# RMSNorm and projection on one core: bf16 cast on GpSimd, bf16 transposes on TensorE, four token tiles per transfer, a software pipeline over pairs of tiles

## The chip, the cores and the metric

The kernel runs on one core of one Trainium2 chip. A core has five engines that run side by side, each with its own instruction queue that is worked off in order: TensorE (PE: matmuls and transposes through its array; weight loads, PEld, overlap them), VectorE (DVE), ScalarE (ACT), GpSimd (POOL), and SyncE (SP), which here only issues DMAs. Sixteen DMA engines move data between HBM and the on-chip memory SBUF; TensorE writes its results to PSUM, from which VectorE and ScalarE read. The metric is the device time of the program in microseconds (us), the median of several runs. A profile of one execution gives a span, the time from the first to the last instruction.

## The reference

```python
batch, seq, dim, out_dim = 16, 1024, 512, 768
rms = np.sqrt(np.mean(x ** 2, axis=-1, keepdims=True) + eps)
x_norm = x / rms * gamma
return np.matmul(x_norm, weight).astype(np.float32)
```

There are 16,384 tokens of 512 f32 values (33.6 MB), a weight of 512x768 f32 (1.57 MB) and an output of 16,384x768 f32 (50.3 MB).

## The kernel before

The tokens are cut into 128 tiles of 128 tokens, one token per partition. Gamma is multiplied into the weight once, which is kept in bf16 as `w_bf` (L56 to L61: SyncE loads both, ScalarE multiplies). The division by the root mean square commutes with the matmul, so it is applied at the end, as the scale `rstd` of each output row.

The loop over tiles (L64 to L95) does this for each tile. SyncE loads `xt_f`, 128x512 f32, 256 KB, 2 KB per partition (L66). ScalarE squares it and accumulates the row sum in `ssq` (L70), and takes the root (L73); VectorE takes the reciprocal (L75). TensorE transposes the tile in four pieces of 128x128, in f32, to PSUM (L80); ScalarE and VectorE in turn copy each piece to SBUF as bf16, `xT` (L81). TensorE multiplies with the weight in two column blocks of 384, four steps in the contracted dimension each (L88). ScalarE scales the first block with `rstd` into `ot` (L94), VectorE the second (L92). SyncE stores `ot`, 384 KB, 3 KB per partition (L95).

The order within each engine's queue is chosen by the scheduler of the tile framework, which interleaves neighbouring tiles. Pools set how far tiles may run ahead: three input tiles (`xin`), three outputs (`outp`), four PSUM tiles for transposes, two for matmul results. All DMAs are issued from SyncE's one queue, in which a DMA that waits for its data or its buffer holds up those behind it.

Of the kernel before, what the change touches and what calls it, by code (L numbers as in the profile page):

```python
# [1 line left out]

# [6 lines left out]
_cc.warn_once_per_call_stack = lambda *a, **k: None  # L9
if hasattr(_cc, "log"):  # L10
    _cc.log.warn_once_per_call_stack = lambda *a, **k: None

F32 = mybir.dt.float32
BF16 = mybir.dt.bfloat16
AF = mybir.ActivationFunctionType


@with_exitstack
def kernel(
    ctx: ExitStack,  # L20
    tc: tile.TileContext,
    x: bass.AP,
    gamma: bass.AP,
    weight: bass.AP,
    eps: float,
    out: bass.AP,
):
    nc = tc.nc
    P = 128

    x = x.flatten_outer_dims()
    out = out.flatten_outer_dims()
    N, D = x.shape
    _, O = out.shape
    K = D // P

    wk = weight.rearrange("(ko ki) o -> ki ko o", ki=P)
    gk = gamma.rearrange("(ko ki) -> ki ko", ki=P)

    singles = ctx.enter_context(tc.tile_pool(name="singles", bufs=1))  # L40
    xin = ctx.enter_context(tc.tile_pool(name="xin", bufs=3))
    work = ctx.enter_context(tc.tile_pool(name="work", bufs=3))
    stats = ctx.enter_context(tc.tile_pool(name="stats", bufs=4))
    xt_pool = ctx.enter_context(tc.tile_pool(name="xt", bufs=3))
    tpsum = ctx.enter_context(tc.tile_pool(name="tpsum", bufs=4, space=bass.MemoryType.PSUM))
    opsum = ctx.enter_context(tc.tile_pool(name="opsum", bufs=2, space=bass.MemoryType.PSUM))
    outp = ctx.enter_context(tc.tile_pool(name="out", bufs=3))

    ident = singles.tile([P, P], F32)
    make_identity(nc, ident)  # L50

    eps_sb = singles.tile([P, 1], F32)
    nc.vector.memset(eps_sb, float(eps))  # L53

    w_f32 = singles.tile([P, K, O], F32)
    nc.sync.dma_start(out=w_f32, in_=wk)  # L56
    g_sb = singles.tile([P, K], F32)
    nc.sync.dma_start(out=g_sb, in_=gk)
    w_bf = singles.tile([P, K, O], BF16)
    for k in range(K):  # L60
        nc.scalar.mul(out=w_bf[:, k, :], in_=w_f32[:, k, :], mul=g_sb[:, k:k + 1])  # L61

    ntiles = N // P
    for m in range(ntiles):  # L64
        xt_f = xin.tile([P, D], F32)
        nc.sync.dma_start(out=xt_f, in_=x[m * P:(m + 1) * P, :])  # L66

        xs = work.tile([P, K, P], BF16)
        ssq = stats.tile([P, 1], F32)
        nc.scalar.activation(out=xs, in_=xt_f.rearrange("p (ko ki) -> p ko ki", ki=P),  # L70
                             func=AF.Square, accum_out=ssq)
        rms = stats.tile([P, 1], F32)
        nc.scalar.activation(out=rms, in_=ssq, func=AF.Sqrt, scale=1.0 / D, bias=eps_sb)  # L73
        rstd = stats.tile([P, 1], F32)
        nc.vector.reciprocal(out=rstd, in_=rms)  # L75

        xT = xt_pool.tile([P, K, P], BF16)
        for k in range(K):
            tp = tpsum.tile([P, P], F32)
            nc.tensor.transpose(out=tp, in_=xt_f.rearrange("p (ko ki) -> p ko ki", ki=P)[:, k, :], identity=ident)  # L80
            nc.vector.tensor_copy(out=xT[:, k, :], in_=tp) if k % 2 else nc.scalar.copy(out=xT[:, k, :], in_=tp)  # L81

        ot = outp.tile([P, O], F32)
        OT = 384
        for oi in range(O // OT):
            ops = opsum.tile([P, OT], F32)
            for k in range(K):
                nc.tensor.matmul(out=ops, lhsT=xT[:, k, :], rhs=w_bf[:, k, oi*OT:(oi+1)*OT],  # L88
                                 start=(k == 0), stop=(k == K - 1))
            oslc = ot[:, oi*OT:(oi+1)*OT]  # L90
            if oi % 2:
                nc.vector.tensor_single_scalar(out=oslc, in_=ops, scalar=rstd, op=mybir.AluOpType.mult)  # L92
            else:
                nc.scalar.mul(out=oslc, in_=ops, mul=rstd)  # L94
        nc.sync.dma_start(out=out[m * P:(m + 1) * P, :], in_=ot)  # L95


# [1 line left out]
_INS = ['x', 'gamma', 'weight', 'eps']  # L99
_OUTS = [((16, 1024, 768), 'float32')]  # L100
#: Inputs that are plain numbers.
_NUMBERS = {'eps': 9.999999747378752e-06}


# [26 lines left out]
```

## Time and profile before

| what | us |
|---|---|
| median of 3 runs | 299.18 |
| the runs | 299.02, 299.18, 301.84 |
| span of the profiled execution | 300.5 |
| TensorE busy | 256.5 (85%) |
| ScalarE busy | 239.1 (80%) |
| VectorE busy | 151.9 (51%) |
| GpSimd busy | 0.7 (0%) |

The page gives each engine's busy time, the DMA queues, and the costliest groups of instructions with their count and mean duration. Other views of the trace give waits by engine and line, the instructions in order of time, and busy time and DMA rate in chosen stretches. Matmuls are pipelined, so a matmul's duration holds latency that the next one overlaps; its cost is read from how far apart the starts of several are. The DMA share is the mean busy share of the 16 DMA engines.

### The profile page before, as it was taken

The numbers are of one execution on the slowest core, as the hardware profiler recorded it, in microseconds if no ns is written. First come the engines' busy times: TensorE is split into PE (matmuls) and PEld (weight loads), VectorE is DVE, ScalarE is ACT, GpSimd is POOL, SyncE is SP. The second block draws the span as 40 slices with busy tenths as digits, with TensorE's granted clock in tenths as the row PEclk, the third lists the DMA queues.
The fourth block names the chain that finished last, engine by engine and source line by source line (L and its number), as shares of the span: only waits on it lengthen the run. The fifth ranks groups of instructions, "written<-read, shape, count | busy, mean of one in ns | idle before, by whom it ended". The sixth has DMA issues, their size and how long they took to land.

```text
span 300.5 us, 5189 instructions
## 1 busy us (share of the span) xinstructions
PE 256.5 (85%) x1536; PEld 153.2 (51%) x1536; DVE 151.9 (51%) x513; ACT 239.1 (80%) x774; POOL 0.7 (0%) x6
## 2 busy tenths in 40 slices
PE   0498799999979999979979989879989889899984
PEld 0155365555545555545545555545555545555542
DVE  0145354646545556546545545645546555556562
ACT  0987569888878888878879878879879879888873
POOL 0000000000000000000000000000000000000000
PEclk9999889999999999999999999999999999999998
DMA  6248869999989999979979989988999999899994
GB/s 230 112 145 277 286 214 318 302 303 314 299 289 323 315 277 327 306 272 312 311 266 306 326 280 301 313 287 292 310 308 285 317 313 303 307 295 305 296 316 164
DMA packets 37948, 85.81 MB, mean 286 GB/s; under 512 B 4640, under 2 KB 4640, under 8 KB 37920
## 3 DMA queue, kind: packets, MB, share of 16 engines
q1 hardware_dynamic: 37920, 85.48, 85.6%
q8 instruction: 12, 0.20, 0.3%
q14 instruction: 16, 0.13, 0.1%
HBM read 35.13 MB, written 50.33 MB: 284 GB/s over the span
## 4 chain that ended last, share of the span: by engine, by line
DMA 46%; PE 43%; ACT 5%; DVE 3%; issue 2%; SPq 1%; ACTq 0%
DMA xt_f<-in_x_dram 44%; PE ops L88 32%; PE tp L80 11%; DVE ot L92 3%; DMA g_sb<-in_gamma_dram 2%; ACT xs L70 1%; ACT ot L94 1%; ACT w_bf L61 1%; ACT rms L73 1%; ACT L73 0%; ACT L61 0%; SPq L95 0%; ACT xT L81 0%; SPq L56 0%; SPq L66 0%
## 5 line engine op out<-in xcount | busy, mean ns | idle before, releaser
L88 PE MATMUL ops<-w_bf,xT 128*128 128x384 bf16 x1024 | 210.2, 330 | 8.3 <-ACT xT L81 4.2
L88 PEld LDWEIGHTS <-xT 128*128 128x128 bf16 x1024 | 98.6, 101 | 70.0 <-ACT xT L81 13.4
L80 PE MATMUL tp<-ident,xt_f 128*128 128x128 f32 x512 | 104.2, 285 | 31.7 <-DMA xt_f<-in_x_dram 31.1
L70 ACT ACTIVATE xs<-xt_f 128x512 bf16<-128x512 f32 x128 | 80.8, 631 | 31.6 <-DMA xt_f<-in_x_dram 30.1
L80 PEld LDWEIGHTS tp<-ident,xt_f 128*128 128x128 f32 x512 | 68.0, 143 | 72.9 <-DMA xt_f<-in_x_dram 45.9
L92 DVE TENSOR_SCALAR ot<-ops,rstd 128x384 f32<-128x384 f32 x128 | 79.1, 618 | 47.8 <-PE ops L88 47.5
L94 ACT ACTIVATE ot<-ops,rstd 128x384 f32<-128x384 f32 x128 | 73.9, 577 | 8.5 <-PE ops L88 2.5
L81 DVE CAST xT<-tp 128x128 bf16<-128x128 f32 x256 | 64.3, 281 | 20.2 <-PE tp L80 19.5
L81 ACT CAST xT<-tp 128x128 bf16<-128x128 f32 x256 | 65.7, 259 | 9.6 <-PE tp L80 2.1
L75 DVE RECIPROCAL rstd<-rms 128x1 f32<-128x1 f32 x128 | 20.9, 163 | 76.5 <-ACT rms L73 76.1
L73 ACT ACTIVATE rms<-ssq,eps_sb 128x1 f32<-128x1 f32 x128 | 37.9, 296 | 0.0
L70 ACT ACTIVATION_READ_ACCUMULATOR xs<-xt_f 128x1 f32 x128 | 24.2, 189 | 0.0
L61 ACT ACT_TABLE_LOAD x1 | 1.3, 1283 | 7.9 <-DMA g_sb<-in_gamma_dram 7.9
L61 ACT ACTIVATE w_bf<-w_f,g_sb 128x768 bf16<-128x768 f32 x4 | 3.4, 922 | 0.0
L73 ACT ACT_TABLE_LOAD x1 | 1.3, 1283 | 0.0
L53 DVE MEMSET eps_sb<- 128x1 f32 x1 | 0.1, 59 | 0.8 <-PEq L112 0.8
masks.py:199 POOL TENSOR_SCALAR_AFFINE_SELECT ident<-ident 128x128 f32<-128x128 f32 x1 | 0.3, 293 | 0.1
masks.py:197 POOL MEMSET ident<- 128x128 f32 x1 | 0.2, 204 | 0.3 <-POOLq L112 0.3
L112 POOL MEMSET const-bfloat16-1.0<- 128x1 bf16 x1 | 0.1, 101 | 0.0
L112 POOL MEMSET const-uint8-127<- 128x1 uint8 x1 | 0.1, 101 | 0.0
L112 POOL MEMSET const-float32-0.0<- 128x1 f32 x1 | 0.1, 98 | 0.2 <-issue 0.2
L112 POOL MEMSET const-float32-1.0<- 128x1 f32 x1 | 0.1, 98 | 0.0
## 6 DMA issues: line engine op xcount, KB each, us to landing
out_dram<-ot SPq DMA_DIRECT2D x128, 384.0 KB, 3.3
xt_f<-in_x_dram SPq DMA_DIRECT2D x128, 256.0 KB, 3.7
w_f<-in_weight_dram SPq DMA_DIRECT2D x1, 1536.0 KB, 6.5
g_sb<-in_gamma_dram SPq DMA_DIRECT2D x1, 2.0 KB, 6.6
```

The source lines that it names most:

```text
L53: nc.vector.memset(eps_sb, float(eps))
L61: nc.scalar.mul(out=w_bf[:, k, :], in_=w_f32[:, k, :], mul=g_sb[:, k:k + 1])
L70: nc.scalar.activation(out=xs, in_=xt_f.rearrange("p (ko ki) -> p ko ki", ki=P), func=AF.Square, accum_out=ssq)
L73: nc.scalar.activation(out=rms, in_=ssq, func=AF.Sqrt, scale=1.0 / D, bias=eps_sb)
L75: nc.vector.reciprocal(out=rstd, in_=rms)
L80: nc.tensor.transpose(out=tp, in_=xt_f.rearrange("p (ko ki) -> p ko ki", ki=P)[:, k, :], identity=ident)
L81: nc.vector.tensor_copy(out=xT[:, k, :], in_=tp) if k % 2 else nc.scalar.copy(out=xT[:, k, :], in_=tp)
L88: nc.tensor.matmul(out=ops, lhsT=xT[:, k, :], rhs=w_bf[:, k, oi*OT:(oi+1)*OT], start=(k == 0), stop=(k == K - 1))
L92: nc.vector.tensor_single_scalar(out=oslc, in_=ops, scalar=rstd, op=mybir.AluOpType.mult)
L94: nc.scalar.mul(out=oslc, in_=ops, mul=rstd)
L112: nc = _bacc.Bacc("TRN2", target_bir_lowering=False, num_devices=1)
```

## The change

A group is now four tiles: partition p holds the four consecutive tokens 4p to 4p+3 of the group's 512, so that a load brings 8 KB in one run per partition (1 MB per DMA) and a store takes 12 KB (1.5 MB). The input pool holds eight groups; the first load is split in two, and the last group is stored in two halves. The order of each queue is the order in which the code is written (`manual_schedule`). Work goes in pairs of tiles, j. GpSimd casts a pair to bf16 (`cast`, L71). ScalarE squares both tiles and takes both roots in one instruction (L77, L80). TensorE transposes the bf16 pair in eight pieces into one bf16 PSUM tile (L90), which VectorE copies in one instruction (L92). The matmuls have column blocks of 512 and 256 (L106); ScalarE scales the first tile's 768 columns (L110), VectorE the second's (L112). In step j of the loop stand: a load six groups ahead (in even steps), the cast of pair j+2, squares and transposes of pair j+1, matmuls and scaling of pair j, and after every second step the store of the group. Gamma is loaded as four rows and transposed on TensorE; the weight is loaded in four DMAs from ScalarE's queue, and VectorE multiplies gamma into it.

```diff
--- before.py
+++ after.py
@@ -33,72 +33,141 @@
     N, D = x.shape
     _, O = out.shape
     K = D // P
+    G = 4
+    NG = N // (P * G)
+    NP = 2 * NG
+    PF = 6
+    SPLITS = [(0, 512), (512, O)]
 
-    wk = weight.rearrange("(ko ki) o -> ki ko o", ki=P)
-    gk = gamma.rearrange("(ko ki) -> ki ko", ki=P)
+
+    xg = x.rearrange("(g p t) d -> g p t d", p=P, t=G)
+    og = out.rearrange("(g p t) o -> g p t o", p=P, t=G)
 
     singles = ctx.enter_context(tc.tile_pool(name="singles", bufs=1))
-    xin = ctx.enter_context(tc.tile_pool(name="xin", bufs=3))
-    work = ctx.enter_context(tc.tile_pool(name="work", bufs=3))
+    xin = ctx.enter_context(tc.tile_pool(name="xin", bufs=PF + 2))
+    xbp = ctx.enter_context(tc.tile_pool(name="xb", bufs=3))
+    junk = ctx.enter_context(tc.tile_pool(name="junk", bufs=2))
     stats = ctx.enter_context(tc.tile_pool(name="stats", bufs=4))
     xt_pool = ctx.enter_context(tc.tile_pool(name="xt", bufs=3))
-    tpsum = ctx.enter_context(tc.tile_pool(name="tpsum", bufs=4, space=bass.MemoryType.PSUM))
-    opsum = ctx.enter_context(tc.tile_pool(name="opsum", bufs=2, space=bass.MemoryType.PSUM))
-    outp = ctx.enter_context(tc.tile_pool(name="out", bufs=3))
+    tpsum = ctx.enter_context(tc.tile_pool(name="tpsum", bufs=2, space=bass.MemoryType.PSUM))
+    opsum = ctx.enter_context(tc.tile_pool(name="opsum", bufs=3, space=bass.MemoryType.PSUM))
+    outp = ctx.enter_context(tc.tile_pool(name="out", bufs=4))
 
-    ident = singles.tile([P, P], F32)
-    make_identity(nc, ident)
+    x_tiles, xb_tiles, rstd_tiles, xT_tiles, o_tiles = {}, {}, {}, {}, {}
 
-    eps_sb = singles.tile([P, 1], F32)
-    nc.vector.memset(eps_sb, float(eps))
+    def load(g, parts=1):
+        xt = xin.tile([P, G, D], F32, name="xt")
+        x_tiles[g] = xt
+        n = G // parts
+        for i in range(parts):
+            nc.sync.dma_start(out=xt[:, i * n:(i + 1) * n, :], in_=xg[g, :, i * n:(i + 1) * n, :])
 
-    w_f32 = singles.tile([P, K, O], F32)
-    nc.sync.dma_start(out=w_f32, in_=wk)
-    g_sb = singles.tile([P, K], F32)
-    nc.sync.dma_start(out=g_sb, in_=gk)
-    w_bf = singles.tile([P, K, O], BF16)
-    for k in range(K):
-        nc.scalar.mul(out=w_bf[:, k, :], in_=w_f32[:, k, :], mul=g_sb[:, k:k + 1])
+    def xpair(j):
+        return x_tiles[j // 2][:, 2 * (j % 2):2 * (j % 2) + 2, :]
 
-    ntiles = N // P
-    for m in range(ntiles):
-        xt_f = xin.tile([P, D], F32)
-        nc.sync.dma_start(out=xt_f, in_=x[m * P:(m + 1) * P, :])
+    def cast(j):
+        xb = xbp.tile([P, 2, D], BF16, name="xb")
+        xb_tiles[j] = xb
+        nc.gpsimd.tensor_copy(out=xb, in_=xpair(j))
 
-        xs = work.tile([P, K, P], BF16)
-        ssq = stats.tile([P, 1], F32)
-        nc.scalar.activation(out=xs, in_=xt_f.rearrange("p (ko ki) -> p ko ki", ki=P),
-                             func=AF.Square, accum_out=ssq)
-        rms = stats.tile([P, 1], F32)
+    def squares(j):
+        ssq = stats.tile([P, 2], F32, name="ssq")
+        for t in range(2):
+            jk = junk.tile([P, D], BF16, name="jk")
+            nc.scalar.activation(out=jk, in_=xpair(j)[:, t, :], func=AF.Square,
+                                 accum_out=ssq[:, t:t + 1])
+        rms = stats.tile([P, 2], F32, name="rms")
         nc.scalar.activation(out=rms, in_=ssq, func=AF.Sqrt, scale=1.0 / D, bias=eps_sb)
-        rstd = stats.tile([P, 1], F32)
+        rstd = stats.tile([P, 2], F32, name="rstd")
         nc.vector.reciprocal(out=rstd, in_=rms)
+        rstd_tiles[j] = rstd
 
-        xT = xt_pool.tile([P, K, P], BF16)
+    def transposes(j):
+        xb = xb_tiles.pop(j)
+        tp = tpsum.tile([P, 2, K, P], BF16, name="tp")
+        for t in range(2):
+            for k in range(K):
+                nc.tensor.transpose(out=tp[:, t, k, :], in_=xb[:, t, k * P:(k + 1) * P], identity=ident)
+        xT = xt_pool.tile([P, 2, K, P], BF16, name="xT")
+        nc.vector.tensor_copy(out=xT, in_=tp)
+        xT_tiles[j] = xT
+
+    def matmuls(j):
+        g, h = j // 2, j % 2
+        if h == 0:
+            o_tiles[g] = outp.tile([P, G, O], F32, name="ot")
+        ot = o_tiles[g]
+        xT = xT_tiles.pop(j)
+        rstd = rstd_tiles.pop(j)
+        for t in range(2):
+            ops = opsum.tile([P, 2, 512], F32, name="ops").rearrange("p a b -> p (a b)")
+            for k in range(K):
+                for lo, hi in SPLITS:
+                    nc.tensor.matmul(out=ops[:, lo:hi], lhsT=xT[:, t, k, :], rhs=w_bf[:, k, lo:hi],
+                                     start=(k == 0), stop=(k == K - 1))
+            dst = ot[:, 2 * h + t, :]
+            if t == 0:
+                nc.scalar.mul(out=dst, in_=ops[:, :O], mul=rstd[:, t:t + 1])
+            else:
+                nc.vector.tensor_single_scalar(out=dst, in_=ops[:, :O], scalar=rstd[:, t:t + 1],
+                                               op=mybir.AluOpType.mult)
+
+    def store(g, lo=0, hi=G):
+        nc.sync.dma_start(out=og[g, :, lo:hi, :], in_=o_tiles[g][:, lo:hi, :])
+
+    with tc.manual_schedule():
+        nc.scalar.preload_act_table(AF.Sqrt)
+        load(0, parts=2)
+
+        g_row = singles.tile([K, P], F32)
+        nc.scalar.dma_start(out=g_row, in_=gamma.rearrange("(ko ki) -> ko ki", ki=P))
+        w_f32 = singles.tile([P, K, O], F32)
         for k in range(K):
-            tp = tpsum.tile([P, P], F32)
-            nc.tensor.transpose(out=tp, in_=xt_f.rearrange("p (ko ki) -> p ko ki", ki=P)[:, k, :], identity=ident)
-            nc.vector.tensor_copy(out=xT[:, k, :], in_=tp) if k % 2 else nc.scalar.copy(out=xT[:, k, :], in_=tp)
+            nc.scalar.dma_start(out=w_f32[:, k, :], in_=weight[k * P:(k + 1) * P, :])
+        for g in range(1, PF):
+            load(g)
 
-        ot = outp.tile([P, O], F32)
-        OT = 384
-        for oi in range(O // OT):
-            ops = opsum.tile([P, OT], F32)
-            for k in range(K):
-                nc.tensor.matmul(out=ops, lhsT=xT[:, k, :], rhs=w_bf[:, k, oi*OT:(oi+1)*OT],
-                                 start=(k == 0), stop=(k == K - 1))
-            oslc = ot[:, oi*OT:(oi+1)*OT]
-            if oi % 2:
-                nc.vector.tensor_single_scalar(out=oslc, in_=ops, scalar=rstd, op=mybir.AluOpType.mult)
-            else:
-                nc.scalar.mul(out=oslc, in_=ops, mul=rstd)
-        nc.sync.dma_start(out=out[m * P:(m + 1) * P, :], in_=ot)
+        ident_f = singles.tile([P, P], F32)
+        make_identity(nc, ident_f)
+        ident = singles.tile([P, P], BF16)
+        nc.vector.tensor_copy(out=ident, in_=ident_f)
+        eps_sb = singles.tile([P, 1], F32)
+        nc.vector.memset(eps_sb, float(eps))
+
+        cast(0)
+        cast(1)
+        squares(0)
+        transposes(0)
+
+        gp = tpsum.tile([P, K], F32, name="tp")
+        nc.tensor.transpose(out=gp, in_=g_row, identity=ident_f[:K, :K])
+        g_sb = singles.tile([P, K], F32)
+        nc.vector.tensor_copy(out=g_sb, in_=gp)
+        w_bf = singles.tile([P, K, O], BF16)
+        for k in range(K):
+            nc.vector.tensor_single_scalar(out=w_bf[:, k, :], in_=w_f32[:, k, :], scalar=g_sb[:, k:k + 1],
+                                           op=mybir.AluOpType.mult)
+
+        for j in range(NP):
+            if j % 2 == 0 and j // 2 + PF < NG:
+                load(j // 2 + PF)
+            if j + 2 < NP:
+                cast(j + 2)
+            if j + 1 < NP:
+                squares(j + 1)
+                transposes(j + 1)
+            matmuls(j)
+            g = j // 2
+            if g == NG - 1:
+                store(g, 2 * (j % 2), 2 * (j % 2) + 2)
+            elif j % 2:
+                store(g)
```

SyncE's queue shows the first place. Rows are in program order; a name such as `xt_f` is the input tile, `ot` the output tile, and the shape is partitions by elements. Before, five loads of one tile stand ahead of the first store, and then a store and a load alternate, with few exceptions:

```order
L56 DMA w_f_86<-in_weight_dram 128x4x768
L58 DMA g_sb<-in_gamma_dram 128x4x1
L66 DMA xt_f<-in_x_dram 128x512 x5
L95 DMA out_dram<-ot 128x768
L66 DMA xt_f<-in_x_dram 128x512
```

In the changed kernel, with the waits for other engines' and earlier DMAs' completions that each row has (DMAHW0 to DMAHW7 are eight completion counters that the DMAs of the program take in turn):

```order
L63 DMA xt<-in_x_dram 128x1024 x2
L63 DMA xt<-in_x_dram 128x2048
L63 DMA xt<-in_x_dram 128x2048 [waits DMAHW0_49]
L63 DMA xt<-in_x_dram 128x2048 [waits DMAHW1_49]
L63 DMA xt<-in_x_dram 128x2048 [waits DMAHW2_49]
L63 DMA xt<-in_x_dram 128x2048 [waits DMAHW3_49]
L63 DMA xt<-in_x_dram 128x2048 [waits DMAHW4_49]
L116 DMA out_dram<-ot 128x3072 [waits DMAHW5_49,DVE_49,Activation_49]
L63 DMA xt<-in_x_dram 128x2048 [waits DMAHW6_49]
```

Seven groups (the first in two halves) are now loaded ahead of the first store, weight and gamma have left the queue, and behind the first store loads and stores alternate with four tiles in each. A row waits for the DMA that took the same counter eight DMAs before it.

VectorE's queue is the second place, some tiles into the loop. `tp` is the PSUM tile of transposes, `ops` that of matmul results. Before:

```order
L75 RECIPROCAL rstd<-rms 128x1
L92 TENSOR_SCALAR ot<-ops,rstd 128x384
L81 CAST xT<-tp 128x128 x2
L75 RECIPROCAL rstd<-rms 128x1
L81 CAST xT<-tp 128x128
L92 TENSOR_SCALAR ot<-ops,rstd 128x384
```

In the changed kernel, from its start:

```order
L82 RECIPROCAL rstd<-rms 128x2
L92 COPY xT<-tp 128x1024
L145 COPY g_sb<-tp 128x4
L148 TENSOR_SCALAR w_bf<-w_f_90,g_sb 128x768 x4
L82 RECIPROCAL rstd<-rms 128x2
L92 COPY xT<-tp 128x1024
L112 TENSOR_SCALAR ot<-ops,rstd 128x768
```

The small casts between the scalings are gone. For each pair the queue now holds three instructions: the reciprocal and the copy of pair j+1, and then the scaling of pair j. The four weight scalings stand behind the first copy.

## Rows read from the trace of the kernel before

**Rows 1.** The page's head and part 1: busy us, share of the span, instructions.

```profile
span 300.5 us, 5189 instructions
PE 256.5 (85%) x1536; PEld 153.2 (51%) x1536; DVE 151.9 (51%) x513; ACT 239.1 (80%) x774; POOL 0.7 (0%) x6
```

**Rows 2.** The page's part 3, DMA queues: packets, MB, share of 16 engines' span.

```profile
q1 hardware_dynamic: 37920, 85.48, 85.6%
```

**Rows 3.** Waits of SyncE's queue: waiting line, awaited: us in total, times, longest.

```profile
SPq L95 <- DVE ot L92: 152.3, 121, 2.9
```

**Rows 4.** Timeline, 150 to 160 us: start, us, engine, line, work [idle before <- awaited].

```profile
151.71 0.95 SPq L66 DMA_DIRECT2D xt_f<-in_x_dram  x1
...
154.47 0.63 ACT L70 ACTIVATE xs<-xt_f 128x512 bf16<-128x512 f32 x1 [1.64 <-DMA xt_f<-in_x_dram]
```

**Rows 5.** The page's part 6, DMA issues: count, KB each, median us to landing.

```profile
out_dram<-ot SPq DMA_DIRECT2D x128, 384.0 KB, 3.3
xt_f<-in_x_dram SPq DMA_DIRECT2D x128, 256.0 KB, 3.7
```

**Rows 6.** Windows: stretch, us, busy PE PEld DVE ACT POOL, clock, DMA share, GB/s.

```profile
4.00:6.00 2.00, 0.00 (x0) 0.00 (x0) 0.00 (x0) 0.00 (x0) 0.00 (x0) 1.00 1.03 416
...
110.00:120.00 10.00, 9.52 (x60) 5.68 (x59) 5.77 (x21) 8.93 (x31) 0.00 (x0) 1.00 0.97 318
160.00:170.00 10.00, 9.61 (x59) 5.68 (x58) 5.93 (x21) 8.76 (x30) 0.00 (x0) 1.00 0.97 324
...
201.00:203.00 2.00, 1.75 (x13) 1.11 (x12) 1.18 (x4) 1.66 (x7) 0.00 (x0) 1.00 1.00 393
```

**Rows 7.** Timeline, 0 to 14 us.

```profile
0.74 0.44 SPq L56 DMA_DIRECT2D w_f<-in_weight_dram  x1
...
13.46 0.82 PE L88 MATMUL ops<-w_bf,xT 128*128 128x384 bf16 x2 [2.83 <-ACT xT L81]
```

**Rows 8.** Timeline, 291 to 301 us, TensorE.

```profile
291.87 0.49 PE L80 MATMUL tp<-ident,xt_f 128*128 128x128 f32 x3
...
294.99 1.50 PE L88 MATMUL ops<-w_bf,xT 128*128 128x384 bf16 x8
```

**Rows 9.** The page's part 5, costliest groups: busy us, mean ns of one | idle before.

```profile
L88 PE MATMUL ops<-w_bf,xT 128*128 128x384 bf16 x1024 | 210.2, 330 | 8.3 <-ACT xT L81 4.2
L88 PEld LDWEIGHTS <-xT 128*128 128x128 bf16 x1024 | 98.6, 101 | 70.0 <-ACT xT L81 13.4
L80 PE MATMUL tp<-ident,xt_f 128*128 128x128 f32 x512 | 104.2, 285 | 31.7 <-DMA xt_f<-in_x_dram 31.1
L70 ACT ACTIVATE xs<-xt_f 128x512 bf16<-128x512 f32 x128 | 80.8, 631 | 31.6 <-DMA xt_f<-in_x_dram 30.1
...
L92 DVE TENSOR_SCALAR ot<-ops,rstd 128x384 f32<-128x384 f32 x128 | 79.1, 618 | 47.8 <-PE ops L88 47.5
L94 ACT ACTIVATE ot<-ops,rstd 128x384 f32<-128x384 f32 x128 | 73.9, 577 | 8.5 <-PE ops L88 2.5
L81 DVE CAST xT<-tp 128x128 bf16<-128x128 f32 x256 | 64.3, 281 | 20.2 <-PE tp L80 19.5
...
L75 DVE RECIPROCAL rstd<-rms 128x1 f32<-128x1 f32 x128 | 20.9, 163 | 76.5 <-ACT rms L73 76.1
L73 ACT ACTIVATE rms<-ssq,eps_sb 128x1 f32<-128x1 f32 x128 | 37.9, 296 | 0.0
L70 ACT ACTIVATION_READ_ACCUMULATOR xs<-xt_f 128x1 f32 x128 | 24.2, 189 | 0.0
...
L61 ACT ACTIVATE w_bf<-w_f,g_sb 128x768 bf16<-128x768 f32 x4 | 3.4, 922 | 0.0
...
masks.py:199 POOL TENSOR_SCALAR_AFFINE_SELECT ident<-ident 128x128 f32<-128x128 f32 x1 | 0.3, 293 | 0.1
masks.py:197 POOL MEMSET ident<- 128x128 f32 x1 | 0.2, 204 | 0.3 <-POOLq L112 0.3
...
L112 POOL MEMSET const-float32-0.0<- 128x1 f32 x1 | 0.1, 98 | 0.2 <-issue 0.2
```

## The prediction

> **What bounds the kernel now.** I read the page's busy shares first. In a span of 300.5 us no engine is full: TensorE is busy 256.5 us and ScalarE 239.1 us [rows 1], and both wait in between. So I went to the transfers. The DMA queue moved 85.48 MB, and its packets filled 85.6% of the 16 engines' span [rows 2]: had they stood end to end they would have taken 0.856 x 300.5 = 257 us, at 332 GB/s. The transfers are the fullest resource, and they too pause for 43 us.
>
> Why they pause is seen in SyncE's queue. It waited 152.3 us in 121 pieces for VectorE's last piece of an output tile, at the store [rows 3]. A load that stands behind such a store can't start, and only three input buffers exist. The timeline shows the price: a load issued at 151.71, and ScalarE idle until 154.47 for an input tile [rows 4]; issue to landing is 3.7 us in the median [rows 5], and three tiles of 2.3 us each (300.5/128) leave little room for that after waits. So before is bound by a loop: compute finishes a tile, the store leaves, the load behind it leaves, compute waits for it.
>
> How fast could the transfers be? The windows tell. Weights and first inputs, reads only, ran at 416 GB/s in 4 to 6 us. In the best 10 us stretch reads and writes mixed ran at 324 GB/s at a share of 0.97, which is 334 at full share; in 201 to 203 us, with no pause, at 393 [rows 6]. So "full" is worth anything between 334 and 393 when mixed.
>
> **The change, part by part.**
>
> Transfers. The same bytes go in a quarter of the DMAs, and a partition's run grows from 2 KB to 8 KB in and from 3 KB to 12 KB out. SyncE's order now has up to seven groups' loads ahead of the first store; after that a load and a store alternate, a load always for a group six later. Each DMA waits for the one eight earlier in the program (the lane in the order's rows), so four loads and four stores, 10 MB, may be in flight: no load that compute needs next stands behind a store that it has yet to fill. So the 43 us of pauses should go nearly whole. What is left is a stream of 85.4 MB. It starts at about 0.7 us [rows 7], and at its end a last DMA needs its landing, 2 to 3 us [rows 5]; I take 3 us for both. At 393 GB/s: 217 + 3 = 220 us. At 334: 256 + 3 = 259. At 416, were writes as fast as reads: 205 + 3 = 208. I take 380 GB/s: near the 393, because the queue is never empty now, as in that window; a little under, because that window is the best of many. That gives 225 + 3 = **228 us**.
>
> TensorE. Per pair of tiles, 16 matmuls now have 512 and 256 columns instead of 384, the same 6144 columns. Eight old ones span 1.50 us, of which the last one's own 0.33 is latency [rows 8, 9]: 0.167 us for each 384 columns, so 2.67 us per pair. The eight transposes become bf16, which no row shows. Above: three f32 ones span 0.49 us, less 0.285 over two, 0.10 each [rows 8, 9]; with weight loads (101 ns, [rows 9]) setting the pace it is the same 0.10. Below: the matmul's pace for 128 columns, 0.167 / 3 = 0.056. So 0.45 to 0.82 per pair, and 3.12 to 3.49 us in all. I take 3.2, nearer the lower end, since a bf16 transpose is a bf16 matmul of 128 columns, which the matmul rows are closest to. Over 64 pairs: 205 us (200 to 223).
>
> ScalarE. It loses half of the copies from PSUM. Per pair: two squares (631 + 189 ns each), one root on two columns (296), one scaling of 768 columns: 922 ns by the row of that size, 1154 by two of the old ones [rows 9]. Sum 2.86 to 3.09 us, 183 to 198 us in all.
>
> VectorE. Per pair one reciprocal (163 ns), one copy of 128x1024 and one scaling of 128x768. The slope between its 128-column and 384-column rows is (618 - 281)/256 = 1.32 ns a column [rows 9], so 1.46 and 1.12 us: 2.75 us, 176 us in all. If two-byte data went twice as fast, 0.6 us less per pair. Either way it hides under TensorE.
>
> GpSimd. It has 64 casts of 128x1024, f32 to bf16, which no row shows either. Its memsets of 128 and of 1 column take 204 and 98 ns, 0.83 ns a column; its select of 128 columns takes 293 ns, 2.3 ns a column with all its fixed cost [rows 9]. So a cast costs 0.9 to 2.3 us, at most 150 us in all, hidden while it stays under TensorE's 3.2 us. Casts run two pairs ahead, so its delay matters only at the start.
>
> Order in a step. Transposes of pair j+1 stand ahead of the matmuls of pair j, so TensorE works while VectorE copies. The copy of j+1 stands ahead of the scaling of j on VectorE, but behind a reciprocal that waits for ScalarE's squares, themselves behind ScalarE's scaling of the pair before. That ring, scaling 0.92, squares and root 1.94, reciprocal 0.16, copy 1.46, half a pair's matmuls 1.34, is 5.8 us and spans two pairs, 2.9 us per pair: just under TensorE's 3.2.
>
> Start and end of compute. Before, the first matmul with weights came at 13.46 us [rows 7], with four scalings on ScalarE in front of it. Now 1.57 MB of weights share the engines with about as much input, 3.1 MB at 400 GB/s, 8 us, plus issue and landing, 2 us, plus a scaling on VectorE, about 1 us: 11 us. At the end a scaling and the last store, 1.1 + 3.3. So compute alone gives 11 + 205 + 4.4 = **220 us** (215 to 239), close under the transfers' 228. All parts but the transfers' stream are therefore hidden, but with little to spare: if the stream ran at 416 GB/s, compute would still hold the time at about 220.
>
> The sum, 228 us, is for a profiled span; before's span of 300.5 stands 1.3 us above the median of its runs, 299.18. I forecast 228 all the same, since the rate is not known that closely.
>
> **The rivals.**
>
> *The mixed stream is no faster than before's.* Place: the DMA engines. If reads and writes in turn are what holds the mixed windows at 334 at full share, larger runs and deeper queues take away only the pauses: 259 us. For it: no 10 us stretch beats 334 [rows 6]. Against: 393 over 2 us with both kinds in flight. The Trainium skill, "DMA: Bandwidth & Descriptors", section "Where 436 GB/s comes from", says that for transfers between HBM and SBUF a limit of about 358 GB/s per core binds; by that rule the stream would take 239 + 3 = 242 us. This trace disagrees for reads alone, 416 GB/s, and says nothing certain for the mix.
>
> *TensorE is the bound.* If bf16 transposes cost 0.10 each, or the weight loads show behind the 256-column matmuls, compute takes 236 to 240 us and the transfers hide. For it: 101 ns of weight load against 0.11 us of a 256-column matmul. Against: weight loads run under the matmuls today, 98.6 us of them inside 210.2 us [rows 9].
>
> *GpSimd is the bound; this one can end slower.* Place: the cast of a pair, on which its transposes wait. From 3.3 us per cast on it sets the pace; at (299 - 15)/64 = 4.4 us per cast the kernel is no faster than before, and at 5 us it takes 15 + 320 = 335 us. Against: 5 us is 4.9 ns a column, twice the dearest row. The Trainium skill, "GPSIMD Engine Reference", section "Elementwise — side-by-side cycle accounting", gives about 2.6 cycles an element at 1.2 GHz, for the engine's elementwise loop; an estimate by it is 2.2 us per cast, which stays hidden. No run so far shows a cast there.
>
> **How the numbers follow.** The forecast (stream at 360 to 410 GB/s, or compute just above it, 215 to 240): 0.65. The mixed stream at its old rate (241 to 262): 0.17. TensorE as the bound (236 to 245): 0.11. GpSimd: 0.07, of which 0.03 beyond 4.4 us. The range that leaves 0.2 out runs from 215, the lower end of compute, to 250; it holds the forecast, TensorE's case and the nearer half of the second. About 1% is what a measurement of this kernel can tell from no change; faster by more than that takes all cases but GpSimd's last: 0.95, the same 0.02, slower 0.03.
>
> **What would show it.** Right: DMA share 0.95 or more in nearly every slice at 370 to 400 GB/s; SyncE's wait for output tiles without loads late behind it; input waits near nothing on TensorE and ScalarE; a cast of 1 to 2.3 us; transposes 0.06 to 0.08 us apart. Wrong: slices full at 334 (second case), slices not full while TensorE never waits (third), or TensorE waiting for GpSimd (fourth). A granted clock well below 1.00, because TensorE waits a little in each pair, would also make it wrong: at half clock the 2.67 us of matmuls double.

## The result and the profile after

The changed kernel takes 222.92 us (221.75 to 223.42 in four runs) against 299.34 us for the kernel before on the same chip: a ratio of 0.745, with a 95% interval of 0.740 to 0.750. The forecast was 228 us, 215 to 250. The time lies in the range; what sets it, TensorE, is not what I named, the transfers.

The page's head, busy shares, the two DMA rows in 40 slices of 5.5 us, the DMA queues and the chain that ended last:

```profile
span 221.0 us, 4062 instructions
PE 198.6 (90%) x1508; PEld 130.8 (59%) x1537; DVE 116.1 (53%) x199; ACT 156.1 (71%) x385; POOL 67.3 (30%) x70
...
DMA  6999379999999999999999999999999999776767
GB/s 199 420 420 425 151 279 395 417 424 423 422 412 428 427 416 429 421 416 420 426 430 426 423 427 429 428 421 426 429 421 425 426 428 415 336 307 291 291 288 285
...
q1 hardware_dynamic: 9504, 83.89, 91.1%
q10 hardware_dynamic: 584, 1.58, 1.8%
...
PE 88%; DMA 7%; issue 1%; DVE 1%; ACTq 1%; ACT 0%
PE ops L106 75%; PE tp L90 13%; DMA w_f<-in_weight_dram 7%; ACTq L126 1%; DVE ot L112 0%; DVE w_bf L148 0%; ACT L119 0%
```

TensorE is busy for 90% of the span, and it is 88% of the chain; before, the fullest resource was the DMA queue with its pauses [rows 1, 2]. The transfers run at 412 to 430 GB/s from slice 8 to slice 34 and then drop to about 290, with the time not yet over: the loads are all in, and stores alone follow TensorE's pace. In slices 5 and 6 they fall to 151 and 279: seven groups are loaded, and the next load stands behind the first store, which leaves only at 28.35 us. A window in the middle (stretch, us, busy PE, PEld, DVE, ACT, POOL, clock, DMA share, GB/s):

```profile
100.00:140.00 40.00, 39.69 (x314) 26.49 (x318) 23.05 (x40) 31.79 (x80) 13.55 (x13) 1.00 1.01 426
```

The costliest groups (busy us, mean ns of one | idle before):

```profile
L106 PE MATMUL ops<-w_bf,xT 128*128 128x256 bf16 (+1 forms) x995 | 178.4, 328 | 10.3 <-DVE w_bf L148 8.8
...
L71 POOL CAST xb<-xt 128x1024 bf16<-128x1024 f32 x64 | 66.6, 1042 | 134.6 <-PE tp L90 125.9
L112 DVE TENSOR_SCALAR ot<-ops,rstd 128x768 f32<-128x768 f32 x64 | 65.1, 1018 | 74.3 <-PE ops L106 74.3
L110 ACT ACTIVATE ot<-ops,rstd 128x768 f32<-128x768 f32 x64 | 57.7, 901 | 53.3 <-PE ops L106 53.3
L77 ACT ACTIVATE jk<-xt 128x512 bf16<-128x512 f32 x128 | 78.7, 619 | 3.1 <-DMA xt<-in_x_dram 3.1
...
L92 DVE COPY xT<-tp 128x1024 bf16<-128x1024 bf16 x64 | 43.0, 671 | 0.3 <-PE tp L90 0.3
```

Everyone else waits for TensorE: GpSimd 125.9 us, VectorE 74.3, ScalarE 53.3. Idle time for inputs on ScalarE is 3.1 us, where it was 30.1 [rows 9]. TensorE's waits all lie at the start, above all for the first cast (6.2 us) and for the four weight pieces (8.8 us).

The steady state in the timeline of TensorE (start us, us):

```profile
121.49 0.61 PE L90 MATMUL tp<-ident,xb 128*128 128x128 bf16 x8
...
121.94 2.76 PE L106 MATMUL ops<-w_bf,xT 128*128 128x512 bf16 x16
...
124.54 0.61 PE L90 MATMUL tp<-ident,xb 128*128 128x128 bf16 x8
...
124.99 2.76 PE L106 MATMUL ops<-w_bf,xT 128*128 128x512 bf16 x15
```

One pair follows the last by 3.05 us: 0.45 us of transposes and 2.60 us of matmuls, with no gap. Over 64 pairs that is 195 us. At its start the chain of waits, in order of time, has

```profile
2.98 16.52 DMA w_f<-in_weight_dram
...
20.20 3.35 PE ops L106 x10
```

The last of the four weight pieces lands at 19.5 us, and the first pair's last matmuls begin at 20.2. With the end from the last scaling on (5.3 us), 195 + 5.3 leaves 20.7 us for the start, where I had 11.

### The profile page after: what moved, and what is told of

It reads as the page before. It is cut to its first block, busy times and chain, and to the rows that moved or that the text cites. A ratio compares the mean times of both kernels' runs of the same rounds, so it can differ in the third digit from the quotient of the medians.

```text
span 221.0 us, 4062 instructions
## 1 busy us (share of the span) xinstructions
PE 198.6 (90%) x1508; PEld 130.8 (59%) x1537; DVE 116.1 (53%) x199; ACT 156.1 (71%) x385; POOL 67.3 (30%) x70
## 4 chain that ended last, share of the span: by engine, by line
PE 88%; DMA 7%; issue 1%; DVE 1%; ACTq 1%; ACT 0%
PE ops L106 75%; PE tp L90 13%; DMA w_f<-in_weight_dram 7%; ACTq L126 1%; DVE ot L112 0%; DVE w_bf L148 0%; ACT L119 0%
## 5 line engine op out<-in xcount | busy, mean ns | idle before, releaser
L106 PE MATMUL ops<-w_bf,xT 128*128 128x256 bf16 (+1 forms) x995 | 178.4, 328 | 10.3 <-DVE w_bf L148 8.8
L106 PEld LDWEIGHTS <-xT 128*128 128x128 bf16 x1024 | 98.3, 99 | 69.3 <-issue 12.0
L71 POOL CAST xb<-xt 128x1024 bf16<-128x1024 f32 x64 | 66.6, 1042 | 134.6 <-PE tp L90 125.9
L112 DVE TENSOR_SCALAR ot<-ops,rstd 128x768 f32<-128x768 f32 x64 | 65.1, 1018 | 74.3 <-PE ops L106 74.3
L110 ACT ACTIVATE ot<-ops,rstd 128x768 f32<-128x768 f32 x64 | 57.7, 901 | 53.3 <-PE ops L106 53.3
L77 ACT ACTIVATE jk<-xt 128x512 bf16<-128x512 f32 x128 | 78.7, 619 | 3.1 <-DMA xt<-in_x_dram 3.1
L90 PE MATMUL tp<-ident,xb 128*128 128x128 bf16 x512 | 40.3, 223 | 6.8 <-POOL xb L71 6.2
L90 PEld LDWEIGHTS <-xb 128*128 128x128 bf16 x512 | 34.9, 100 | 15.0 <-POOL xb L71 6.7
L92 DVE COPY xT<-tp 128x1024 bf16<-128x1024 bf16 x64 | 43.0, 671 | 0.3 <-PE tp L90 0.3
L77 ACT ACTIVATION_READ_ACCUMULATOR jk<-xt 128x1 f32 x128 | 24.4, 190 | 0.0
L80 ACT ACTIVATE rms<-ssq,eps_sb 128x2 f32<-128x2 f32 x64 | 18.9, 295 | 2.1
## 6 DMA issues: line engine op xcount, KB each, us to landing
w_f<-in_weight_dram ACTq DMA_DIRECT2D x4, 384.0 KB, 12.3
```

The source lines that it names most:

```text
L71: nc.gpsimd.tensor_copy(out=xb, in_=xpair(j))
L77: nc.scalar.activation(out=jk, in_=xpair(j)[:, t, :], func=AF.Square, accum_out=ssq[:, t:t + 1])
L90: nc.tensor.transpose(out=tp[:, t, k, :], in_=xb[:, t, k * P:(k + 1) * P], identity=ident)
L92: nc.vector.tensor_copy(out=xT, in_=tp)
L106: nc.tensor.matmul(out=ops[:, lo:hi], lhsT=xT[:, t, k, :], rhs=w_bf[:, k, lo:hi], start=(k == 0), stop=(k == K - 1))
L110: nc.scalar.mul(out=dst, in_=ops[:, :O], mul=rstd[:, t:t + 1])
```

## The experiments

**The weights first.** Is it TensorE's chain, with its late start, that sets the time, or the stream?

```diff
         for k in range(K):
-            nc.scalar.dma_start(out=w_f32[:, k, :], in_=weight[k * P:(k + 1) * P, :])
+            nc.sync.dma_start(out=w_f32[:, k, :], in_=weight[k * P:(k + 1) * P, :])
```

> Theory A (the changed kernel is bound by TensorE's steady 3.05 us per pair, after a start in which the weights, sharing the DMA engines with the input loads, land only at 19.5 us): with the weights issued from SyncE's queue between the first group and the second, they land behind 2.6 MB, 6.2 us at 420 GB/s plus 2 to 3, so at about 9 us; the first pair's matmuls end at about 11 instead of 23 us, and the whole kernel gains what comes earlier, 9 to 12 us: 211 to 214 us. Theory B (the stream of transfers, as the prediction had it, is the bound): the same bytes in the same stream, within 1%: 221 to 225 us.

212.93 us (212.84 to 212.97), 10 us less, as theory A had it. The first matmuls with weights and the chain that ended last:

```profile
8.46 2.27 PE L106 MATMUL ops<-w_bf,xT 128*128 128x512 bf16 x6
```

```profile
PE 91%; issue 3%; DMA 2%; POOL 1%; DVE 0%; SPq 0%; POOLq 0%
```

The chain is TensorE's, as in the changed kernel, and only its start has moved. The same bytes, now all in SyncE's queue, end earlier, which theory B did not allow. This version beats both kernels: ratio 0.711 (0.708 to 0.713) to the kernel before.

**The stream alone.** TensorE's work is lightened in w_first: of the matmuls on the last 256 columns three of four steps are left out, so those columns of the output are incomplete.

```diff
-                for lo, hi in SPLITS:
+                for lo, hi in SPLITS[:2 if k == 0 else 1]:
...
-                                     start=(k == 0), stop=(k == K - 1))
+                                     start=(k == 0), stop=(k == K - 1 or lo > 0))
```

> The changed kernel with the weights sent early (as in w_first), and of the matmuls on the last 256 columns only one of the four steps in the contracted dimension is done, so the output is left incomplete there; TensorE's work falls to about 2.4 us per pair, so that the transfers alone can bound. Theory A (long runs in a full queue stream at 425 GB/s): 85.4 MB / 425 GB/s = 201 us plus 3: 203 to 207 us with the DMA share at 1 throughout. Theory B (the mix of reads and writes holds at 380 GB/s or less once stores never pause): 228 us or more, slower than w_first's 213, which is impossible unless the missing matmuls speed the stores' demand; so B is shown by any time at or above 212.

211.91 us, above theory A's range and 0.1 under the bound at which I would have read B. The windows and the DMA issues (KB each, us to landing) tell why:

```profile
6.00:20.00 14.00, 12.01 (x76) 6.83 (x77) 8.56 (x16) 8.98 (x25) 6.65 (x7) 1.00 1.02 424
...
100.00:150.00 50.00, 40.08 (x286) 22.28 (x283) 27.59 (x48) 36.92 (x93) 16.64 (x16) 1.00 1.01 427
...
205.80:209.80 4.00, 0.00 (x0) 0.00 (x0) 0.00 (x0) 0.00 (x0) 0.00 (x0) 0.50 0.04 18
```

```profile
out_dram<-ot SPq DMA_DIRECT2D x31, 1536.0 KB, 20.1
xt<-in_x_dram SPq DMA_DIRECT2D x31, 1024.0 KB, 22.1
```

TensorE waits (40.1 us busy of 50) and the queue is full, since a store takes 20.1 us to land. The mix of reads and writes streams at 427 GB/s, so B's 380 or less is out. What my sum lacked is above all the end: the last 4 us run at 18 GB/s and a share of 0.04, less than one of the 16 engines. The trace's packet records there are packets of 6 KB, 0.23 us each, from 206.1 us on each starting only when the one before is done. I read that as one engine that ends the kernel while the others are idle; why it lags is open. The transfers' own bound is therefore about 212 us, one us under w_first: the two bounds nearly meet.

**Short runs.** Does the length of the runs make the rate?

```diff
-    xg = x.rearrange("(g p t) d -> g p t d", p=P, t=G)
-    og = out.rearrange("(g p t) o -> g p t o", p=P, t=G)
+    xg = x.rearrange("(g t p) d -> g p t d", p=P, t=G)
+    og = out.rearrange("(g t p) o -> g p t o", p=P, t=G)
```

> The same DMAs of four tiles each, but with a partition holding tokens p, p+128, p+256, p+384 of the group, so that runs are 2 KB in and 3 KB out as in the kernel before. Theory A (TensorE bounds, and the transfers' rate comes from a queue that is never empty): the rate stays at 380 to 425 GB/s, transfers stay hidden: 221 to 227 us. Theory B (the length of the runs makes the rate): the stream falls back to 334 GB/s, 256 + 3 us, and bounds the kernel: 255 to 265 us.

219.50 us (219.44 to 219.70): not slower, but 3.4 us faster than the change. Its window and its weight transfers:

```profile
100.00:150.00 50.00, 50.00 (x399) 33.07 (x397) 28.84 (x49) 39.90 (x100) 16.68 (x16) 1.00 1.04 412
```

```profile
w_f<-in_weight_dram ACTq DMA_DIRECT2D x4, 384.0 KB, 8.2
```

The rate is 412 GB/s, 3% less than with long runs, and TensorE still never waits. The weights land in 8.2 us in the median, in the changed kernel in 12.3. The weights' runs are 3 KB in both; beside loads in 2 KB runs they get a larger part of the engines than beside loads in 8 KB runs. Whether the engines take runs from the two queues in turn I have not tested. At the end a part of the gain is lost: the last scaling begins at 209.99 us, 5.7 earlier than in the changed kernel, but the slower stream then has stores left, and 7.7 us pass to the end of the span instead of 5.3.

The same with the lightened TensorE, and the weights early:

> As stream_long, with runs of 2 KB in and 3 KB out. Theory A (the rate of a full queue depends little on the runs: 411 GB/s was seen in short_runs): 208 us plus 3: 209 to 214 us. Theory B (short runs are what held the kernel before at 334 GB/s): 255 us or more.

218.90 us, against 211.91 with long runs: 3%, again some 5 us above my range for the same kind of end. The middle:

```profile
100.00:150.00 50.00, 39.12 (x279) 21.86 (x278) 25.90 (x45) 35.26 (x90) 15.60 (x15) 1.00 1.04 412
```

So long runs are worth 7 us to the stream, and where TensorE sets the pace only the 2.4 us at the end of short_runs.

**One DMA per token tile.** Short runs as above, and every load and store in four pieces:

```diff
-    def load(g, parts=1):
+    def load(g, parts=4):
...
-        nc.sync.dma_start(out=og[g, :, lo:hi, :], in_=o_tiles[g][:, lo:hi, :])
+        for i in range(lo, hi):
+            nc.sync.dma_start(out=og[g, :, i, :], in_=o_tiles[g][:, i, :])
...
-        load(0, parts=2)
+        load(0)
```

> The changed kernel with one DMA per token tile again (256 KB in, 384 KB out, runs of 2 and 3 KB), 128 loads and 128 stores, everything else as in the change. Theory A (order and prefetch made the gain, not the size of a transfer): like short_runs, 217 to 224 us. Theory B (few large transfers are needed: with eight completion counters only eight DMAs, 2.6 MB, can be in flight, which drains in 6.2 us, and each group then pays 2 us of latency): 32 x 8.2 + 20, about 260 us or more than 235.

224.21 us (223.94 to 224.76), 2% above short_runs, just over the upper edge of theory A. GpSimd now waits for inputs (us in total, times, longest), and in the second half the chain that ended last is of stores (start us, us):

```profile
POOL xb L71 <- DMA xt<-in_x_dram: 49.3, 23, 3.7
```

```profile
125.13 6.57 DMA out_dram<-ot
...
131.76 6.58 DMA out_dram<-ot
...
178.45 6.87 DMA out_dram<-ot
```

```profile
60.00:100.00 40.00, 39.69 (x310) 26.36 (x314) 23.36 (x40) 31.76 (x81) 13.91 (x14) 1.00 1.03 392
```

Up to 125 us TensorE stays full, while the stream runs at 392 GB/s and the lead of the loads shrinks; from there to 185 us nine stores in a row set the pace, 6.6 us each. That fits what theory B described, eight DMAs with 2.6 MB in flight, at a much lower price than its 260 us: 2.6 MB in 6.6 us are 397 GB/s. I did not change the number in flight by itself. The size of the transfers, and with it the number of bytes in flight, is worth 5 us out of 76.

**How far ahead the loads run.**

```diff
-    PF = 6
+    PF = 1
```

> Loads run one group ahead instead of six, so each load is issued behind the store of the group before. Theory A (the kernel before was held by loads issued late behind stores, and the prefetch is what removed its pauses): a load lands 8 us after the store in front of it leaves (2.5 MB at 425 GB/s plus 2 us), then cast 1.0, transposes 0.6, copy 0.7, two pairs 6.1, scaling 1.1: 17.5 us from store to the next store but one, 8.7 us per group, 280 us plus the start: 280 to 300 us, with the input waited for on GpSimd and the DMA share down at 0.65 to 0.75. Theory B (long runs and few large DMAs are what removed the pauses): no change beyond 2%, 220 to 227 us.

538.1 us. Theory B is out, and A is right in kind but far too low. Windows, waits (in total, times, longest) and two stores and a pair in the timeline:

```profile
251.00:256.50 5.50, 5.50 (x22) 2.84 (x21) 0.86 (x2) 2.27 (x7) 0.53 (x1) 0.50 0.01 3
257.00:259.70 2.70, 2.70 (x19) 1.43 (x16) 1.40 (x3) 0.90 (x1) 0.00 (x0) 1.00 0.50 209
259.70:267.00 7.30, 0.02 (x1) 0.00 (x0) 1.02 (x1) 0.68 (x3) 0.55 (x1) 0.75 0.77 282
```

```profile
POOL xb L71 <- DMA xt<-in_x_dram: 454.8, 33, 17.6
...
PE tp L90 <- POOL xb L71: 242.9, 31, 8.4
```

```profile
250.59 1.03 PE L90 MATMUL tp<-ident,xb 128*128 128x128 bf16 x8 [7.96 <-POOL xb L71]
...
251.42 5.25 PE L106 MATMUL ops<-w_bf,xT 128*128 128x512 bf16 x16
...
257.80 0.34 SPq L116 DMA_DIRECT2D out_dram<-ot  x1
...
274.81 0.34 SPq L116 DMA_DIRECT2D out_dram<-ot  x1
```

Two things were missing in my price. The transposes of pair j+1 stand ahead of the matmuls of pair j on TensorE, so the store of a group waits for the load of the next one, and the load after that waits behind this store. The ring closes in one group, not two: 17.0 us from store to store (257.80 to 274.81). And TensorE, idle for some 8 us in each turn, finds its granted clock at 0.50 (1.2 GHz) for the next pair, whose 16 matmuls take 5.25 us, and at 1.00 (2.4 GHz) for the one after. In all TensorE is busy for 285.9 us, where the changed kernel has 198.6. With two groups ahead:

> Loads two groups ahead instead of six. ahead_one showed a ring: store of a group, load behind it 8.1 us to landing, cast 1.0, transposes 1.0, matmuls of the pair before, scaling, next store. With two groups ahead the same ring, 8.1 + 1.1 + 1.0 + 2.6 + 1.4 = 14.2 us, spans two groups. Theory A (the ring sets the pace): 7.1 us per group against 6.1 of TensorE's own, 227 + 20: 245 to 260 us, more where the granted clock falls. Theory B (one group of slack is enough to hide a landing): 221 to 226 us.

265.46 us, a little above theory A's range. The depth of the loads is worth 43 us from two groups to six, more than any other part that was taken away.

**Without the cast.** TensorE transposes the f32 input, with one f32 PSUM tile and one copy per token tile.

```diff
-        xb = xb_tiles.pop(j)
-        tp = tpsum.tile([P, 2, K, P], BF16, name="tp")
+        xT = xt_pool.tile([P, 2, K, P], BF16, name="xT")
         for t in range(2):
+            tp = tpsum.tile([P, K, P], F32, name="tp")
             for k in range(K):
-                nc.tensor.transpose(out=tp[:, t, k, :], in_=xb[:, t, k * P:(k + 1) * P], identity=ident)
-        xT = xt_pool.tile([P, 2, K, P], BF16, name="xT")
-        nc.vector.tensor_copy(out=xT, in_=tp)
+                nc.tensor.transpose(out=tp[:, k, :], in_=xpair(j)[:, t, k * P:(k + 1) * P], identity=ident_f)
+            nc.vector.tensor_copy(out=xT[:, t, :, :], in_=tp)
...
-        cast(0)
-        cast(1)
...
-            if j + 2 < NP:
-                cast(j + 2)
```

> The changed kernel without the cast: TensorE transposes the f32 input as before the change (one f32 PSUM tile and one copy per token tile), GpSimd does nothing in the loop. Theory A (TensorE is the bound, and the bf16 cast takes work from it): a pair costs 2.60 us of matmuls and eight transposes of 0.10, 3.4 us, 0.36 us more than the 3.05 of the changed kernel, over 64 pairs 23 us: 242 to 248 us. Theory B (the cast only moves work, the gain is all from transfers and order): 221 to 226 us.

248.87 us (248.39 to 249.42), 26 us more, a little above theory A's range. In its timeline eight transposes span 1.04 us where the bf16 ones span 0.61. Behind it stand its window, its copies and its stores:

```profile
152.59 1.04 PE L90 MATMUL tp<-ident_f,xt 128*128 128x128 f32 x8
...
153.47 1.79 PE L105 MATMUL ops<-w_bf,xT 128*128 128x512 bf16 x10
```

```profile
100.00:140.00 40.00, 40.00 (x280) 28.29 (x278) 27.07 (x45) 28.37 (x72) 0.00 (x0) 1.00 1.00 377
```

```profile
L91 DVE CAST xT<-tp 128x512 bf16<-128x512 f32 x128 | 81.3, 676 | 0.0
...
out_dram<-ot SPq DMA_DIRECT2D x31, 1536.0 KB, 6.1
```

The start of the transposes to the first matmul is 0.88 us (152.59 to 153.47) against 0.45, and 64 x 0.43 = 27.5 us, near the 26 measured. TensorE is full. But look at the DMA share: 1.00, at 377 GB/s. At 1.31 MB per pair TensorE's pace of 3.48 us asks for just 377. A share of 1.00 is here no sign that the DMA engines are the bound; a store lands in 6.1 us, not in the 20.1 of the full queue.

**The cast twice.**

```diff
+        xd = junk.tile([P, 2, D], BF16, name="xd")
+        nc.gpsimd.tensor_copy(out=xd, in_=xpair(j))
         nc.gpsimd.tensor_copy(out=xb, in_=xpair(j))
```

> GpSimd casts every pair twice, once into a tile that nobody reads. Theory A (GpSimd is hidden, two pairs ahead): 2.1 us per pair stay under TensorE's 3.05, only the first pair comes 1 us later, and that is hidden behind the weights: 221 to 225 us, no change. Theory B (the cast holds the transposes, directly or because GpSimd's traffic to SBUF slows VectorE): one more us in each of 64 pairs or a part of it, 230 us or more, with longer VectorE instructions.

223.14 us (222.77 to 223.26), no change, as in theory A. GpSimd is busy 131.0 us instead of 67.3 and hidden.

**Buffers alone, in the kernel before.**

```diff
-    xin = ctx.enter_context(tc.tile_pool(name="xin", bufs=3))
+    xin = ctx.enter_context(tc.tile_pool(name="xin", bufs=12))
...
-    outp = ctx.enter_context(tc.tile_pool(name="out", bufs=3))
+    outp = ctx.enter_context(tc.tile_pool(name="out", bufs=6))
```

> The kernel before with 12 input buffers instead of 3 and 6 output buffers instead of 3, nothing else by hand. Theory A (before was held by input loads that start late for want of buffers, behind stores): input waits nearly vanish, and what is left is TensorE's own work, 1.74 us per tile (8 x 0.167 + 4 x 0.10), 223 us, plus start and end of 13.5 + 5: 240 to 250 us. Theory B (before was held by the mixed transfers at 334 GB/s): 257 to 262 us, with the DMA share near 1. Theory C (the engines' orders hold each other, buffers do not matter): 290 to 300 us.

285.77 us (283.88 to 287.96), ratio 0.952 (0.945 to 0.958): none of the three. The input waits halve, to

```profile
ACT xs L70 <- DMA xt_f<-in_x_dram: 18.2, 27, 1.4
...
PE tp L80 <- DMA xt_f<-in_x_dram: 16.2, 12, 9.1
```

from 30.1 on ScalarE and 31.1 on TensorE, and 15 us are gained of the 50 to 60 that theory A expected. In ScalarE's queue the scheduler now puts a tile's square ahead of that tile's copies, by up to eight tiles early in the run and by none after tile 90, where it waits for a load that has just been issued and can hold up the copies behind it. From the issue of a load to the start of its square 4.1 us pass in the median, in the kernel before 3.8. So the edit did not bring the loads forward against their first use, and it does not decide theory A for the kernel before. That reading comes from counting the instructions in the trace and from waits such as 0.43 us at 154.37; I did not test it apart. Deeper buffers without a written order give a fifth of the gain.

**The weights behind the first pair, the last pair in two stores.** Two edits to w_first in one run: the weights one half group earlier, and the last pair stored tile by tile.

```diff
-        load(0, parts=2)
+        x_tiles[0] = xin.tile([P, G, D], F32, name="xt")
+        nc.sync.dma_start(out=x_tiles[0][:, :2, :], in_=xg[0, :, :2, :])
...
+        nc.sync.dma_start(out=x_tiles[0][:, 2:, :], in_=xg[0, :, 2:, :])
...
-            if g == NG - 1:
-                store(g, 2 * (j % 2), 2 * (j % 2) + 2)
+            if j == NP - 1:
+                store(g, 2, 3)
+                store(g, 3, 4)
+            elif g == NG - 1:
+                store(g, 0, 2)
```

> w_first with the weights one half group earlier (behind the first pair only) and the last pair stored tile by tile. Theory A (TensorE's chain bounds from start to end): the first matmuls come about 1 us earlier and the last store is half as large and lands 0.5 to 1 us sooner: 210.5 to 212 us. Theory B (w_first already stands at the transfers' bound, the full stream with one DMA engine lagging at its end that stream_long showed at 212): no change, 212.5 to 213.5 us.

215.49 us (215.23 to 216.53), 2.6 us slower than w_first. Neither theory: the weights do come earlier, but the second pair's input now lands behind them, and its transposes stand ahead of the first matmuls:

```profile
12.01 1.04 PE L90 MATMUL tp<-ident,xb 128*128 128x128 bf16 x8 [4.22 <-POOL xb L71]
```

The first matmuls start at 12.84 us instead of 8.46. It is the order that closed the ring of ahead_one: the first matmuls need two pairs. The other edit did what theory A expected of it: from the start of the last scaling to the end of the span 5.15 us pass (208.25 to 213.4), in w_first 5.65 (205.55 to 211.2).

## Why the prediction was right, and where it was not

**What bounds the kernel before: right in kind, shown only in the changed kernel.** Late loads behind stores make such pauses there: ahead_one and ahead_two bring them back. In the kernel before itself the loop is argued from its trace; that buffers alone would not undo it (285.77) I had not seen. The two rows of [rows 4] that I put side by side belong to different tiles: counted through the trace, the square at 154.47 waits for the load issued at 149.13.

**The rate of the stream: wrong.** This step failed: "full" is worth anything between 334 and 393 when mixed, and the 380 GB/s taken from it. The same mix of reads and writes ran at 427 GB/s once the queue was full, which gives 200 us instead of 225. Against that, start and end of the stream cost more than the 3 us that I gave them: stream_long takes 212 us. My 334 "at full share" [rows 6] took the DMA share for a measure of fullness. It isn't: f32_transposes shows a share of 1.00 at 377 GB/s with TensorE as the bound, stream_long 1.01 at 427. So the second rival, the mixed stream at its old rate, rested on a misread row; stream_short shows 412 GB/s even with the old runs. The limit of about 358 GB/s that the Trainium skill has in "DMA: Bandwidth & Descriptors", section "Where 436 GB/s comes from", did not bind here either: 426 GB/s over 40 us on this one core.

**TensorE: the right step, a little high.** Matmuls 2.60 us per pair (2.67 in my sum), transposes 0.45, the lower end of 0.45 to 0.82; 3.05 where I took 3.2, 195 us instead of 205.

**The start: wrong, 20.7 us instead of 11.** I let weights and inputs share the engines half and half. In the first 20 us 7.2 MB moved (360 GB/s), of which the weights are 1.6, not a half, and the last weights landed at 19.5 us; w_first, which takes the sharing away, gave back 10 us.

**The sum.** Compute was 11 + 205 + 4.4 = 220 us in the prediction and is 20.7 + 195 + 5.3 = 221 in the trace: two errors of 10 us cancel. The forecast of 228 stood on the transfers, which were not the bound. That it came within 5 us of the time is luck: the transfers' sum was too high by 16 us against stream_long, and the time of the changed kernel comes from another sum. By the signs that I wrote down it was the third case, slices that are not full (35 to 40) while TensorE never waits, at another price. The granted clock, another of these signs, stayed at 0.996. The sentence that compute would hold the time at about 220 if the stream ran at 416 GB/s is what happened; the rival "TensorE is the bound" named the engine, at 236 to 245 us, for reasons (transposes of 0.10, weight loads that show) that did not come.

**ScalarE, VectorE, GpSimd: hidden, as forecast.** ScalarE needs 156 us, not 183 to 198: two squares start 0.62 us apart (121.19 and 121.81 in the timeline), so the read of the accumulator lies under the next one. VectorE's copy takes 671 ns for 1024 columns where the slope gave 1460: the two-byte copy runs about twice as fast as the four-byte one, which takes 676 ns for 512 columns in f32_transposes, the lower case that I had kept. The cast takes 1042 ns, in my 0.9 to 2.3, and cast_twice shows its cover. The 2.6 cycles an element of the Trainium skill's "GPSIMD Engine Reference", section "Elementwise — side-by-side cycle accounting", would have made it 2.2 us; the section puts that figure down to two inputs, which I had passed over, and for this one-input cast the trace shows 1.02 ns a column, under half of that.

**Where the 76 us came from**, by taking one part away at a time: loads six groups ahead instead of two, 43 us; the bf16 cast, 26 us; four tiles per DMA, 5 us with short runs; long runs, minus 3 us here, because they delay the weights. The parts do not add up, since each is measured with the others in place. The written order of the queues and the new split of ScalarE's and VectorE's work were not taken away by themselves, so their share is open.

## What to carry to other kernels

Judge a stream of transfers by its rate with a full queue and by the time from issue to landing (16 to 20 us for a store of 1.5 MB in the two kernels with lightened TensorE, 6 to 13 us where TensorE or a ring set the pace), not by the share of time in which packets are in flight. In a software pipeline, write down which instruction stands ahead of which on the in-order engine: here the transposes ahead of the matmuls turned a shallow prefetch into a ring of 17 us, and a well meant earlier load into a loss. Look at the start by itself: sharing the DMA engines between the first inputs and the weights cost 10 us, and a change of one word gave them back.

## What was unexpected of the hardware

The DMA share stays at 1.00 while the rate falls from 427 to 377 GB/s at the pace of another engine. A full stream ended with 4 us at 18 GB/s, one packet behind the other. Two queues with different runs do not share evenly: weights in 3 KB runs landed in 12.3 us beside loads in 8 KB runs and in 8.2 us beside 2 KB runs. And beside a cast on GpSimd, VectorE's scaling of a weight piece from SBUF to SBUF took about twice its 620 ns: with two casts per pair 1.37 and 1.20 us for the two of four that met a cast, 953 ns in the mean, and with one cast per pair 1.21 and 1.26 us in short_runs. Its instructions that read PSUM kept their 1018 and 672 ns:

```profile
12.47 1.37 DVE L150 TENSOR_SCALAR w_bf<-w_f,g_sb 128x768 bf16<-128x768 f32 x1 [2.74 <-DMA w_f<-in_weight_dram]
...
19.39 0.62 DVE L150 TENSOR_SCALAR w_bf<-w_f,g_sb 128x768 bf16<-128x768 f32 x1 [2.27 <-DMA w_f<-in_weight_dram]
```

```profile
L114 DVE TENSOR_SCALAR ot<-ops,rstd 128x768 f32<-128x768 f32 x64 | 65.1, 1018 | 74.7 <-PE ops L108 74.7
...
L150 DVE TENSOR_SCALAR w_bf<-w_f,g_sb 128x768 bf16<-128x768 f32 x4 | 3.8, 953 | 7.5 <-DMA w_f<-in_weight_dram 7.5
```
